# Hybrid recurrent decoder step: head loads on Pool's queue, one matmul per sample state instead of two, LayerNorm pieces on ACT and DVE alone

## The chip, the cores and the metric

The kernel runs on one core of a Trainium2 chip. The metric is the device time of one execution in microseconds. Three runs of the kernel before took 2374.15, 2374.71 and 2378.41 us; the median is 2374.71 us. The profiled execution, from which all durations below come, took 2384.39 us.

A core has five engines that each work through their own queue in program order: TensorE (PE, matrix products), VectorE (DVE), ScalarE (ACT), GpSimd (POOL) and SyncE (SP). SP and POOL also issue most DMAs here. An engine, or a queue, whose next instruction waits for something holds everything behind it.

## The reference, cut to what matters

One layer of a decoder is computed for a prompt (512 tokens) and for 8 sample tokens with states of their own. One projection `u @ w_in` (2048 x 19464) gives the columns of three mixers and of the gates:

- A: a gated linear recurrence, 8 heads with 128 x 128 states;
- B: retention, 4 heads with 256 x 256 states;
- C: mLSTM, 4 heads with 256 x 256 states.

Each branch is normalised per head, multiplied by a gate and projected by `w_branch`; the three are merged with sigmoid gates, projected by `w_out`, and `LayerNorm(alpha * x + out)` is the result. For a sample token of B (and, with other factors, C) one step is

```
s_new = chunk_dec[:, None, None] * s + jnp.einsum('bshk,bshv->bhkv', ..., vc)
o     = jnp.einsum('bthk,bhkv->bthv', ..., s_new)      # q^T S of the state after its update
```

So each of 8 tokens x 4 heads x 2 mixers = 64 states of 256 x 256 is loaded, updated, stored and multiplied by its q vector. The last step of the layer is `(h - mu) * rsqrt(var + eps) * ln_g + ln_b` over rows of 2048.

## The kernel before, in words

Dense products. All float32 matrices are split into a high and a low part (`hi`, `lo`, type float32r), and a product is hi*hi + hi*lo + lo*hi. The weights stream through three 1 MB buffers `R`; ACT makes `hi`, DVE makes `lo`. Work is cut into items: 24 matmuls of 128x260 for a Strassen product of `w_in`, 48 for an item of a plain product (the first three column blocks, `w_branch`, `w_out`). In most Strassen units two column blocks of the weights are summed by DMA into `TT`: SP loads the first, POOL adds the second with an accumulating DMA (`one.hook(2, ...)` in `strassen_unit`).

Side work. The heads of A, B and C, and the samples, are generators. `dense` emits a few matmuls, yields, and `side_step` then lets three queues of generators (`prepq`, `scanq`, `sampq`) each emit a step, if a model clock (`Clock`, written when the program is built) says that the step's inputs are there and that DVE and ACT are not more than 2.0 and 2.5 us behind the end of the current item (`clk.next`, set in `dense` to 2.87 us after the item's start, L735). So the order of each engine's instructions is fixed when the program is built, by the clock's costs (L152 to 163).

Loads of the side work. A finished column block is parked in DRAM (`parked`, POOL's queue). `ld` (L782) brings the block of one head back into a slot of `SL`, a buffer of 16 slots of 128x520; `b_head` loads the rotary tables (L1167) and `lds_` in `bc_samp` the sample states (L1265). All three issue on SP's queue, where the loads of `R` and of the first half of `TT` stand as well. POOL's queue has the stores, the parked blocks, the `TT` accumulations and the broadcast of the samples' v (`SL<-vs`).

Samples of B and C, `bc_samp` (L1244). A 256x256 state lies in a slot as 128 partitions x two halves of 256 columns; rows 2p and 2p+1 of the state share partition p. ACT multiplies v by k for both halves (`SL<-SL,ks`), DVE updates both halves, POOL stores the state, and PE forms q^T S as two float32 products of 128x256, one for each half, whose left side is q masked to the token's column (`qmask`, tile `qmt`), all 16 of a head accumulated in `os`.

Last LayerNorm, `norm_rows` (L1767). Rows are finished in two halves (two chunks of 128 rows each). Each chunk is cut into three or four pieces; a piece is scaled by ACT, multiplied by `g` on DVE, and `b` is added on POOL for the first two pieces and on DVE for the rest. The first half is a generator in `sampq`, emitted beside the last matmuls; the second half comes after them, interleaved with `norm_samples`.

## Time and profile before

| | |
|---|---|
| median of three runs | 2374.71 us (2374.15 to 2378.41) |
| profiled execution, device time | 2384.39 us |
| its span, first to last instruction | 2382.5 us |
| PE busy | 2318.9 us (97%) |
| DVE busy | 1603.2 us (67%) |
| ACT busy | 1031.3 us (43%) |
| POOL busy | 490.8 us (21%) |
| mean granted TensorE clock | 0.992 |

How to read it: `PD` are the accumulators of the dense products, `s` and `os` those of the side work and of the samples. A float32 matmul leaves two records in the trace, a float32r matmul or a transpose one; so the 128 products of the samples of B and C stand as 256 records. All engine operations are recorded by one wrapper and so have one line, L165; DMAs have L142, accumulating DMAs L143. The A heads run from about 180 to 800 us of the span, B from 800 to 1300, C from 1280 to 1793; the branch projections follow until about 2125, the output projection until 2353.6, and the rest is the LayerNorm of the second half.

### The profile page before, as it was taken

What the parts mean: (1) busy time and instruction counts of PE and PEld (TensorE: products, weight loads), DVE (VectorE), ACT (ScalarE), POOL (GpSimd) and SP (SyncE); (2) the same over time, 40 slices, a digit from 0 to 9 for tenths busy, and PEclk for the clock granted to TensorE, in tenths of its full rate; (3) what the DMA queues carried; (4) which work ended last, traced back from release to release, by engine and by line L of the source; (5) the groups of instructions that cost most, each with busy time, mean ns of one, the idle gap of its engine ahead of it and who ended that gap; (6) DMA issues with size and microseconds to landing.
All of it is one profiled execution on the core that took longest, in us unless ns stands there. A gap on an engine that the chain in (4) does not pass through costs nothing.

```text
span 2382.5 us, 45461 instructions
## 1 busy us (share of the span) xinstructions
PE 2318.9 (97%) x18677; PEld 2240.8 (94%) x18677; DVE 1603.2 (67%) x2571; ACT 1031.3 (43%) x1611; POOL 490.8 (21%) x653
## 2 busy tenths in 40 slices
PE   7999999999999999999999999999999999999995
PEld 7999999999999999999999899898999999999994
DVE  5777777787778868677777666767676534553336
ACT  4344445445545444454445545554554422222222
POOL 2022221323222132222122222212221100002002
PEclk9999999999999999999999999999999999999997
DMA  6367765647566576767767988889796767755221
GB/s 178 116 158 186 196 161 170 184 151 219 149 204 167 182 213 189 223 216 205 234 184 207 187 246 203 221 200 241 169 252 173 225 201 256 253 192 199 89 72 72
DMA packets 404690, 449.26 MB, mean 189 GB/s; under 512 B 16993, under 2 KB 356865, under 8 KB 402945
## 3 DMA queue, kind: packets, MB, share of 16 engines
q1 hardware_dynamic: 313664, 312.77, 42.3%
q0 software_dynamic: 90384, 133.38, 24.2%
q8 instruction: 147, 2.41, 0.4%
q14 instruction: 63, 0.51, 0.1%
q10 hardware_dynamic: 432, 0.20, 0.0%
HBM read 362.98 MB, written 83.28 MB: 187 GB/s over the span
## 4 chain that ended last, share of the span: by engine, by line
PE 61%; DMA 3%; DVE 1%; ACT 1%; issue 0%; POOL 0%; SPq 0%; DVEq 0%; POOLq 0%; ACTq 0%
PE PD L165 54%; PE s L165 4%; PE os L165 3%; DMA R<-in_w_in_dram 1%; DVE SL L165 1%; DMA out_dram<-SL 0%; DMA R<-in_w_branch_dram 0%; DMA TT<-in_w_in_dram 0%; ACT hi L165 0%; DVE lo L165 0%; ACT SL L165 0%; ACT TT L165 0%; DVE sdd L165 0%; DVE R L165 0%; DVE fmv L165 0%
## 5 line engine op out<-in xcount | busy, mean ns | idle before, releaser
L165 PE MATMUL PD<-XZ,hi 128*128 128x260 f32 x9920 | 1430.0, 285 | 13.3 <-ACT hi L165 10.0
L165 PEld LDWEIGHTS PD<-XZ,hi 128*128 128x128 f32 x9920 | 1282.7, 189 | 30.8 <-ACT hi L165 12.0
L165 DVE TENSOR_TENSOR lo<-R,hi 128x1024 fp32r<-128x1024 f32 (+1 forms) x540 | 646.1, 1198 | 381.2 <-ACT hi L165 161.6
L165 PE MATMUL PD<-XZ,lo 128*128 128x260 f32 x4944 | 799.4, 284 | 0.2 <-DVE lo L165 0.2
L165 ACT ACTIVATE hi<-R 128x1024 fp32r<-128x1024 f32 (+1 forms) x541 | 558.1, 1051 | 499.4 <-PE PD L165 254.8
L165 PEld LDWEIGHTS PD<-XZ,lo 128*128 128x128 f32 x4944 | 679.9, 189 | 5.5 <-issue 4.3
L165 ACT ACTIVATE SL<-PD 128x260 f32<-128x260 f32 x304 | 115.2, 381 | 424.3 <-PE PD L165 363.9
L165 POOL COPY smp<-SL 128x8 f32<-128x8 f32 x104 | 93.1, 895 | 535.3 <-ACT SL L165 344.2
L165 DVE TENSOR_TENSOR R<-R,R 128x1024 f32<-128x1024 f32 x146 | 178.0, 1219 | 6.4 <-DMA R<-in_w_in_dram 6.2
L165 DVE TENSOR_TENSOR SL<-SL 128x256 f32<-128x256 f32 (+9 forms) x315 | 146.4, 501 | 32.9 <-PE s L165 26.5
L165 PE MATMUL PD<-X,hi 128*128 128x260 f32 x1168 | 165.1, 287 | 0.3 <-ACT hi L165 0.3
L165 DVE TENSOR_TENSOR SL<-PD,SL 128x260 f32<-128x260 f32 x219 | 93.0, 425 | 99.4 <-PE PD L165 89.8
L165 PEld LDWEIGHTS PD<-X,hi 128*128 128x128 f32 x1168 | 148.4, 188 | 5.0 <-issue 4.1
L165 PE MATMUL s<-SL 128*128 128x64 f32 (+5 forms) x912 | 147.3, 298 | 0.0
L143 POOL DMA_DIRECT2D TT<-in_w_in_dram x56 | 90.2, 1610 | 272.7 <-DMA TT<-in_w_in_dram 245.5
L165 PEld LDWEIGHTS s<-SL 128*128 128x128 f32 (+1 forms) x912 | 125.0, 187 | 6.2
L165 ACT ACTIVATE SL<-SL 128x520 f32<-128x520 f32 (+5 forms) x156 | 85.2, 565 | 66.4 <-DVE SL L165 64.9
L142 POOL DMA_DIRECT2D out_dram<-SL x100 | 61.0, 614 | 217.9 <-DVE SL L165 196.3
L165 POOL TENSOR_TENSOR rstd<-rva,half 128x4 f32<-128x4 f32 (+3 forms) x35 | 45.2, 1292 | 247.5 <-DVE rva L165 247.4
L165 DVE TENSOR_TENSOR lo<-TT,hi 128x1024 fp32r<-128x1024 f32 x73 | 88.8, 1217 | 3.1 <-ACT hi L165 3.0
L165 DVE TENSOR_TENSOR R<-R 128x1024 f32<-128x1024 f32 x73 | 88.9, 1217 | 0.0
L165 PE MATMUL PD<-X,lo 128*128 128x260 f32 x584 | 84.7, 285 | 0.0
(213 smaller groups left out, 1416.7 us busy)
## 6 DMA issues: line engine op xcount, KB each, us to landing
R<-in_w_in_dram SPq DMA_DIRECT2D x150, 1024.0 KB, 6.3
TT<-in_w_in_dram SPq DMA_DIRECT2D x56, 512.0 KB, 6.4
TT<-in_w_in_dram POOLq DMA_DIRECT2D x56, 512.0 KB, 6.5
R<-in_w_branch_dram SPq DMA_DIRECT2D x24, 1024.0 KB, 6.5
out_dram<-SL POOLq DMA_DIRECT2D x88, 256.0 KB, 5.5
R<-in_w_out_dram SPq DMA_DIRECT2D x16, 1024.0 KB, 5.4
pk_g<-SL POOLq DMA_DIRECT2D x48, 260.0 KB, 4.7
SL<-pk_g SPq DMA_DIRECT2D x48, 260.0 KB, 5.9
```

What stands on the lines that cost most here:

```text
L142: return f(out=out, in_=in_)
L143: return f(out=out, in_=in_, accum_op=accum_op)
L165: return f(*a, **kw)
```

## The change

- `ld`, the rotary tables and the sample states are issued on POOL's queue instead of SP's: 32 + 40 + 40 loads of blocks and tables and 64 of states, 176 in all.
- In `bc_samp` the two halves are joined before the product: after the update ACT forms half 0 times q0 (per partition scalar) in a free slot, DVE adds half 1 times q1, and PE makes one 128x256 product whose left side is the constant mask `e8`. `qmask` goes for B and C.
- `norm_rows` has four pieces of 512 columns a chunk; DVE does both the product with `g` and the sum with `b`, ACT scales one piece ahead, and POOL has no piece. The generator's steps come due sooner (`clk.latest = 0.0`, `yield 1` instead of `yield 2`).
- Two numbers of the model clock: a float32 matmul costs twice as much, and an item of a plain product has 5.74 us to its end instead of 2.87 (Strassen items keep 2.87). Both change where side work is emitted.

```diff
-                    t = max(0.06, 0.00046 * n) if a[2].dtype == F32R else max(0.06, 0.00085 * n)
+                    t = max(0.06, 0.00046 * n) if a[2].dtype == F32R else 2 * max(0.06, 0.00085 * n)
...
-            clk.next = clk.pe + 2.87
+            clk.next = clk.pe + it.span
...
     def ld(nm, k, pre=False):
         s = sl()
-        SY.dma_start(out=v3(s[:, 0:S], 2), in_=d2(ptile(f"{nm}{k}"))[:, :, 0:256], pre=pre)
+        G.dma_start(out=v3(s[:, 0:S], 2), in_=d2(ptile(f"{nm}{k}"))[:, :, 0:256], pre=pre)
...
-            SY.dma_start(out=cs2[i][:, 0:S], in_=rope[i, :, 0:S])
+            G.dma_start(out=cs2[i][:, 0:S], in_=rope[i, :, 0:S])
...
-            SY.dma_start(out=v3(st[:, 0:512], 2), in_=state_in[0, b, h].rearrange("(p t) v -> p t v", t=2), pre=True)
+            G.dma_start(out=v3(st[:, 0:512], 2), in_=state_in[0, b, h].rearrange("(p t) v -> p t v", t=2), pre=True)
...
-        qm = [qmask(q[e], e) for e in range(2)]
...
-                fr(tm)
                 yield 1
                 for b in bs:
-                    st = lds.pop(b)
-                    for e in range(2):
-                        T.matmul(po[0:NS, 0:256], qm[e][:, b, :], st[:, e * 256:(e + 1) * 256],
-                                 start=(b == 0 and e == 0), stop=(b == 7 and e == 1))
+                    i = (b % 2) * 256
+                    act(out=tm[:, i:i + 256], in_=lds[b][:, 0:256], func=AF.Copy, scale=q[0][:, b:b + 1])
+                yield 1
+                for b in bs:
+                    i, st = (b % 2) * 256, lds.pop(b)
+                    V.scalar_tensor_tensor(out=tm[:, i:i + 256], in0=st[:, 256:512], scalar=q[1][:, b:b + 1],
+                                           in1=tm[:, i:i + 256], op0=MUL, op1=ADD)
                     fr(st)
+                yield 1
+                for b in bs:
+                    i = (b % 2) * 256
+                    T.matmul(po[0:NS, 0:256], e8[:, b, :], tm[:, i:i + 256], start=(b == 0), stop=(b == 7))
+                fr(tm)
                 yield 1
...
-        for c in range(2):
-            hh = H[:, c0 + c, :]
-            for q0, q1, e in (((0, 672, G), (672, 1344, G), (1344, 2048, V)) if c0 + c < 3 else
-                              ((0, 640, G), (640, 1152, G), (1152, 1600, V), (1600, 2048, V))):
-                qq = slice(q0, q1)
-                act(out=hh[:, qq], in_=hh[:, qq], func=AF.Identity, scale=r[:, c:c + 1], bias=nm[:, c:c + 1])
-                V.tensor_tensor(out=hh[:, qq], in0=hh[:, qq], in1=g[:, qq], op=MUL)
-                e.tensor_tensor(out=hh[:, qq], in0=hh[:, qq], in1=b[:, qq], op=ADD)
-                SY.dma_start(out=y_p[0, (c0 + c) * 128:(c0 + c + 1) * 128, qq], in_=hh[:, qq])
-                yield 2
+        pieces = [(c, slice(q0, q0 + 512)) for c in range(2) for q0 in range(0, D, 512)]
+
+        def scaled(c, qq):
+            hh = H[:, c0 + c, qq]
+            act(out=hh, in_=hh, func=AF.Identity, scale=r[:, c:c + 1], bias=nm[:, c:c + 1])
+
+        scaled(*pieces[0])
+        for i, (c, qq) in enumerate(pieces):
+
+            if i + 1 < len(pieces):
+                scaled(*pieces[i + 1])
+            hh = H[:, c0 + c, qq]
+            V.tensor_tensor(out=hh, in0=hh, in1=g[:, qq], op=MUL)
+            V.tensor_tensor(out=hh, in0=hh, in1=b[:, qq], op=ADD)
+            SY.dma_start(out=y_p[0, (c0 + c) * 128:(c0 + c + 1) * 128, qq], in_=hh)
+            clk.latest = 0.0
+            yield 1
```

How it moves instructions, at three places.

PE's queue at the end of the samples of the last C head, before (`PD` are dense matmuls, `os<-SL,qmt` the samples' products, x4 is two states):

```order
L165 MATMUL PD_126<-X_85,hi_121 128x260 x3
L165 MATMUL os<-SL,qmt 8x256 x4
L165 MATMUL PD_126<-X_85,hi_121 128x260 x13
L165 MATMUL PD_126<-X_85,lo_123 128x260 x8
L165 MATMUL PD_125<-XZ,hi_122 128x260 x3
```

and in the change:

```order
L165 MATMUL PD_127<-XZ,hi_120 128x260 x16
L165 MATMUL PD_127<-XZ,lo_123 128x260 x2
L165 MATMUL os<-SL,e_91 8x256 x2
L165 MATMUL PD_127<-XZ,lo_123 128x260 x6
L165 MATMUL PD_128<-X_85,hi_121 128x260 x16
```

Two states now take two products instead of four, and the left side is the constant mask.

SP's queue in the samples of the last but one C head, before (`R` are the weights, `SL<-in_state_mlstm_c` the states, `pk_mo` and `pk_mz` parked blocks):

```order
L142 DMA TT<-in_w_in_dram 128x8x128
L142 DMA SL<-in_state_mlstm_c_dram 128x512
L142 DMA SL<-pk_mo_12045 128x2x256
L142 DMA SL<-pk_mo_12146 128x2x256
L142 DMA SL<-pk_mz_12266 128x2x256
L142 DMA SL<-pk_mz_12374 128x2x256
L142 DMA SL<-in_state_mlstm_c_dram 128x512 x3
L142 DMA R_116<-in_w_in_dram 128x8x256
L142 DMA R_117<-in_w_in_dram 128x8x256
```

and POOL's queue in the samples of the last C head in the change (`pk_g` are parked gates, `out_dram<-SL` stores):

```order
L142 DMA SL<-pk_mo_13343 128x2x256
L142 DMA SL<-pk_mo_13466 128x2x256
L142 DMA SL<-pk_mz_13617 128x2x256
L142 DMA SL<-pk_mz_13728 128x2x256
L143 DMA TT<-in_w_in_dram 128x8x128
L142 DMA out_dram<-SL 128x512
L142 DMA pk_g_12_17483<-SL 128x520
L142 DMA SL<-vs_111 128x512
L142 DMA SL<-in_state_mlstm_c_dram 128x512 x2
L142 DMA SL<-vs_111 128x512
L142 DMA SL<-in_state_mlstm_c_dram 128x512
L142 DMA pk_g_13_17602<-SL 128x520
```

SP keeps the weights, the first halves of `TT` and the gates; the states and blocks now stand between POOL's stores and accumulations.

DVE's queue from the last tile of the output projection to the second half's statistics, before:

```order
L165 BN_STATS AT<-SL 128x6 x2
L165 TENSOR_TENSOR SL<-SL,lng 128x704
L165 TENSOR_TENSOR SL<-SL,lnb 128x704
L165 TENSOR_TENSOR SL<-SL,lng 128x672 x2
L165 TENSOR_TENSOR SL<-SL,lng 128x704
L165 TENSOR_TENSOR SL<-SL,lnb 128x704
L165 BN_AGGR fmv<-AT 128x2 x2
```

In the change ten operations of 512 columns, five with `lng` and five with `lnb` in turn, stand between the same two rows; these are the last of them:

```order
L165 TENSOR_TENSOR SL<-SL,lng 128x512
L165 TENSOR_TENSOR SL<-SL,lnb 128x512
L165 BN_AGGR fmv<-AT 128x2 x2
L165 TENSOR_SCALAR rva<-fmv 128x2
L165 SCALAR_TENSOR_TENSOR nm<-fmv,rstd 128x2
```

Three of the first half's eight pieces now stand ahead of the last tile, where two of six stood before.

More of the change, by code (lines that the diff above doesn't have):

```diff
@@ L327, in tile_hybrid_step @@
     e8 = const.tile([128, 8, 8], F32, name="e8")
-    qmt = const.tile([128, 2, 8, 8], F32, name="qmt")
+    qmt = const.tile([128, 8, 8], F32, name="qmt")
     ones = const.tile([128, 1], F32, name="ones")
@@ L425, in ralloc @@
         return r
+    span = [5.74]
     class Item:
@@ L433, in __init__ @@
             self.late = False
+            self.span = span[0]
             self.part = None
@@ L500, in strassen_unit @@
     def strassen_unit(col, deint, fin):
+        span[0] = 2.87
         src = w_in[0][:, col:col + 256]
@@ L654, in classical_rows @@
     def classical_rows(src, rws, xf, fin, pre=None):
+        span[0] = 5.74
         kt = 8 * rws
@@ L806, in put_ys, with qmask @@
         V.scalar_tensor_tensor(out=ysm[:, 8 * br + k, :], in0=psum, scalar=gains[:, br, k:k + 1], in1=z, op0=MUL, op1=MUL)
-    def qmask(q, e):
-        t = qmt[:, e]
-        V.tensor_tensor(out=t, in0=e8, in1=q.unsqueeze(2).to_broadcast([128, NS, 8]), op=MUL)
-        return t
+    def qmask(q):
+        V.tensor_tensor(out=qmt, in0=e8, in1=q.unsqueeze(2).to_broadcast([128, NS, 8]), op=MUL)
+        return qmt
     def samp_silu(i0, n):
@@ L1023, in a_samp @@
         hb = {}
-        qm = qmask(q, 0)
+        qm = qmask(q)
         def get(b0):
```

## The prediction

> **What bounds the kernel now.** I read the page's busy times first, then the stretches, then PE's waits, and last the queue of SP.
>
> ```profile
> span 2382.5 us, 45461 instructions
> PE 2318.9 (97%) x18677; PEld 2240.8 (94%) x18677; DVE 1603.2 (67%) x2571; ACT 1031.3 (43%) x1611; POOL 490.8 (21%) x653
> PE 61%; DMA 3%; DVE 1%; ACT 1%; issue 0%; POOL 0%; SPq 0%; DVEq 0%; POOLq 0%; ACTq 0%
> ```
>
> PE is busy for 97% of the span, and the chain that ended last is followed back over two thirds of the span with 61 of its 66 points on PE. The stretches show where the rest lies; columns are PE, weight loads, DVE, ACT, POOL, clock, DMA share, GB/s (the last row has PE alone of the engines).
>
> ```profile
> 50.00:450.00 400.00, 395.47 (x3308) 392.11 (x3307) 301.19 (x454) 178.73 (x288) 84.08 (x106) 1.00 0.59 160
> 450.00:800.00 350.00, 349.60 (x2889) 340.05 (x2889) 275.59 (x474) 171.61 (x303) 100.21 (x128) 1.00 0.62 176
> 800.00:1300.00 500.00, 498.95 (x3905) 472.16 (x3903) 368.53 (x552) 236.43 (x355) 125.24 (x172) 1.00 0.72 213
> 1300.00:1800.00 500.00, 488.96 (x3769) 457.17 (x3768) 348.78 (x595) 258.18 (x404) 112.70 (x146) 0.99 0.87 210
> 1800.00:2335.00 535.00, 530.29 (x4413) 527.58 (x4412) 250.70 (x379) 150.84 (x192) 39.66 (x69) 1.00 0.56 182
> 2354.00:2383.00 29.00, 1.12 (x4) 0.52 0.32 123
> ```
>
> PE idles 1 us in the B heads (800 to 1300), 11 us in the C heads (1300 to 1800), and 28 us after its last product. The clock is full. So a microsecond taken off PE's queue is a microsecond of the span, as long as DVE (70 to 79% busy there) and the loads keep up.
>
> **The products of the samples.** 64 of 128 products go.
>
> ```profile
> L165 PE MATMUL os<-SL,qmt 128*8 128x256 f32 x256 | 61.9, 380 | 0.0
> 1080.31 1.89 PE L165 MATMUL os<-SL,qmt 128*8 128x256 f32 x8
> 1082.13 0.98 PE L165 MATMUL PD<-XZ,lo 128*128 128x260 f32 x6
> ```
>
> The timeline has eight records, four products, from 1080.31 until the dense matmuls go on at 1082.13: 1.82 / 4 = 0.455 us each, 64 x 0.455 = 29.1 us. By the group's busy time it is 61.9 / 2 = 31.0. I take 29.1.
>
> **What they are replaced by.** For each of 64 states one ACT operation and one DVE operation of 256 columns; 16 `qmask` operations go.
>
> ```profile
> L165 ACT ACTIVATE SL<-SL,ks 128x256 f32<-128x256 f32 x128 | 62.2, 503 | 2.5 <-DMA SL<-vs 0.4
> L165 DVE SCALAR_TENSOR_TENSOR SL<-SL 128x256 f32<-128x256 f32 x64 | 22.9, 418 | 0.1
> L165 DVE TENSOR_TENSOR qmt<-e,smp 128x64 f32<-128x64 f32 x24 | 4.6, 218 | 0.0
> ```
>
> ACT gets 64 x 0.503 = 32.2 us, DVE 64 x 0.418 - 16 x 0.218 = 23.3 us. In 800 to 1800 DVE is idle for 1000 - 368.5 - 348.8 = 283 us and ACT for 505, so both fit under PE. They aren't free: a product now waits for a chain state update, ACT, DVE, and a `lo` operation queued behind a new one comes 0.4 us later. Without that cover all of DVE's 23.3 us would show. I take 4 us, between 0 and 12 (half of DVE's addition); nearer 0, because DVE has ten times the room.
>
> **SP's queue without the loads.** This is where the C heads' 11 us come from.
>
> ```profile
> SPq L142 <- DMA out_dram<-SL: 77.6, 17, 11.4
> 1605.33 1.37 SPq L142 DMA_DIRECT2D SL<-pk_mo  x2
> 1611.95 18.01 SPq L142 DMA_DIRECT2D SL<-in_state_mlstm_c_dram  x3
> 1630.01 1.05 SPq L142 DMA_DIRECT2D R<-in_w_in_dram  x2
> 1618.12 11.45 DMA out_dram<-SL
> 1630.01 6.43 DMA R<-in_w_in_dram
> 1636.47 1.06 ACT hi L165
> PE PD L165 <- ACT hi L165: 8.1, 4, 3.7
> ```
>
> A load of a state waits 11.45 us until the store out of its slot has landed, the weights behind it in the queue leave at 1630.01 and land 6.43 us later, ACT's `hi` comes at 1636.47, and PE has waited. In 1300 to 1800 PE has four such waits, 8.1 us, the longest 3.7. In the change the wait stands on POOL's queue and the weights leave when their buffer is free. I take 7 us, between 0 and 8.1.
>
> The Trainium skill, "DMA: Bandwidth & Descriptors", section "Issuing engines are not separate DMA queues", speaks against this: transfers from all issuing engines share the same 16 engines, and another issuer saves only issue time. By it this term is 0 and the rest of the sum stands; no run here shows it yet, since the rows above show a wait in a queue and not a want of bandwidth, though the DMA share of 0.87 allows either.
>
> **POOL's queue with them.** 176 loads come to a queue that waits on its own things.
>
> ```profile
> L143 POOL DMA_DIRECT2D TT<-in_w_in_dram x56 | 90.2, 1610 | 272.7 <-DMA TT<-in_w_in_dram 245.5 <-issue 16.5 <-DMA SL<-in_state_mlstm_c_dram 10.6
> L142 POOL DMA_DIRECT2D SL<-vs x48 | 26.5, 554 | 9.7 <-DVE SL L165 4.3 <-issue 3.7 <-PE s L165 0.7
> SL<-vs POOLq DMA_DIRECT2D x48, 256.0 KB, 5.8
> SL<-in_state_ret_dram SPq DMA_DIRECT2D x32, 256.0 KB, 7.6
> TT<-in_w_in_dram POOLq DMA_DIRECT2D x56, 512.0 KB, 6.5
> ```
>
> POOL's load is 176 x 0.554 = 97.5 us more, on 490.8: 25% of the span. A load of this size lands 5.8 us after its issue there and 7.6 on SP, where it follows 1 MB of weights; but POOL runs with PE and SP a little ahead of it, so I count arrival as equal. What is behind a waiting load: `TT` accumulations, and parked blocks whose slots are not short. What is ahead of a load: an accumulation that waits 272.7 / 56 = 4.9 us for its first half. In the changed order few loads stand right behind one. I take 1 us, between 0 and 6; a gain is excluded, since PE waits for none of these loads now.
>
> **The clock's numbers.** The dearer float32 matmul moves side work to places nearer to its inputs; that risk is in the 4 us above. The longer plain item lets the output projection's transposes of the second tile stand right behind the item's last matmul, where six matmuls of the next item stood between; the first tile's have stood so already.
>
> ```profile
> PE s L165 <- ACT TT L165: 2.5, 7, 0.4
> ```
>
> Seven times 0.36 us more: 2.5 us, between 2 and 4.
>
> **The LayerNorm.** From the last tile on, DVE is the chain.
>
> ```profile
> 2354.47 0.88 DVE L165 TENSOR_TENSOR SL<-SL,lng 128x704 f32<-128x704 f32 x1
> 2360.04 2.17 DVE L165 TENSOR_TENSOR SL<-SL,lnb 128x704 f32<-128x704 f32 x1
> 2362.14 1.02 DVE L165 BATCH_NORM_AGGREGATE fmv<-AT 128x2 f32<-128x96 f32 x2
> 2364.25 0.16 DVE L165 SCALAR_TENSOR_TENSOR nm<-fmv,rstd 128x2 f32<-128x2 f32 x1 [0.89 <-POOL rstd L165]
> 2378.59 0.62 DVE L165 TENSOR_TENSOR SL<-SL,lnb 128x448 f32<-128x448 f32 x1
> L165 DVE TENSOR_TENSOR SL<-SL 128x512 f32<-128x512 f32 x88 | 58.2, 684 | 1.4 <-ACT SL L165 1.4
> ```
>
> An operation of 704 columns takes 0.88 us alone and 2.17 beside POOL's `lnb`; POOL's pieces save DVE little. Before: 2354.47 to 2362.14, 7.7 us for the first half's rest; in the change ten operations of 512 at about 0.70 from start to start, 7.0. Second half, before: 2364.25 to 2379.21, 15.0 us. In the change: ACT's first piece 0.8, sixteen at 0.70, and the samples' small operations, about 2 us: 14.0. So 1.5 us less, between 0 and 3.
>
> **The sum.** -29.1 + 4 - 7 + 1 + 2.5 - 1.5 = -30.1 us on a span of 2382.5, so about 2352. The profiled execution's own time is 2384.4, the runs' median 2374.7, 10 us below it; the difference is taken from the median: 2374.7 - 30.1 = 2344.6, forecast **2345 us**. By the bounds: best -31.0 + 0 - 8.1 + 0 + 2 - 3 = -40.1, 2335; worst -29.1 + 12 + 0 + 6 + 4 + 0 = -7.1, 2368.
>
> **The rivals.**
>
> *The queue move is worth nothing*: the late weights were late for bandwidth. For it the DMA share of 0.87 in the C heads against 0.72 in B; against it the same 210 GB/s in both and the queue rows above. Then -23.1: 2352.
>
> *DVE becomes the bound in the samples*: with 23.3 us more it stands at 74% on average, but its work comes in bursts, and PE's queue waits in order. For it the chain of two more engines ahead of each product; against it only 1 us of PE idle at 74% in the B heads and 0.4 us at 79% in the A heads. All of DVE's addition showing: -29.1 + 23.3 + 2.5 - 1.5 = -4.8, 2370, no change or barely faster.
>
> *Slower: accumulations late on POOL's queue.* Each of 56 `TT` sums gets 176 / 56 = 3.1 loads ahead of it, 1.7 us; issued and landed it takes 1.6 + 6.5 = 8.1 us, and its first reader stands four items later. Four items of 24 matmuls at 68.37 / 569 = 0.12 us (2.88 us an item; both rows below) are 11.5 us, less the 4.9 us that it waits already: the slack is gone in many units. If each passes 1.7 us to PE, 56 x 1.7 = 95 us are added: 2440. It decides for slower from 30 / 1.7 = 18 of 56 on. Against it: ACT's `hi` waits for that DMA twice in the whole span, 1.4 us in all, and most loads don't stand right ahead of an accumulation.
>
> ```profile
> 1805.55 68.37 PE PD L165 x569
> ACT hi L165 <- DMA TT<-in_w_in_dram: 1.4, 2, 1.2
> ```
>
> **Chances.** Forecast 0.70, the queue move worth nothing 0.20, DVE the bound 0.05, accumulations late 0.05. The first two are faster whatever their size. What a measurement of this kernel can tell from no change is about 0.2%, 4.7 us; DVE's case lies at that edge and is shared. Faster 0.91, same 0.04, slower 0.05. Range 2333 to 2362: the forecast's bounds, with the first rival inside and the upper end cut where costs would all have to be at their worst.
>
> **What would show it.** PE's `os` products: 128 records of 128x256 where 256 were, about 30 us less busy. SP's row for waits on `out_dram<-SL` gone, and PE's idle time in the C heads down from 11 to a few us; were the first gone and the second not, the bandwidth rival is right. A row of ACT or PE waiting for `TT<-in_w_in_dram` of tens of us would show the slower rival. DVE's `lng` and `lnb` at 0.68 us each, and 1.5 us less from PE's last transposes to the end. The forecast is wrong if PE's idle time between 100 and 1800 grows by over 10 us.

## The result, and the profile after

| | before | after |
|---|---|---|
| median, same chip, four runs each | 2374.43 us (2372.87 to 2378.41) | 2441.98 us (2430.65 to 2447.98) |
| ratio | | 1.0276, 95% interval 1.0236 to 1.0316 |
| profiled execution / its span | 2384.4 / 2382.5 us | 2440.6 / 2438.8 us |
| mean granted TensorE clock | 0.992 | 0.983 |

The change is slower by 2.8%, 66 us; the forecast was 2345, 30 us faster. The head of the page of the changed kernel, and the engines of its chain:

```profile
span 2438.8 us, 45203 instructions
PE 2317.3 (95%) x18549; PEld 2247.7 (92%) x18549; DVE 1622.7 (67%) x2633; ACT 1058.4 (43%) x1678; POOL 570.9 (23%) x821
...
PE 77%; DMA 13%; DVE 4%; issue 3%; ACT 2%; POOL 1%; SPq 0%; ACTq 0%; DVEq 0%; POOLq 0%
```

DMA's share of the chain rises from 3 to 13%. The same stretches as before the change (PE, weight loads, DVE, ACT, POOL, clock, DMA share, GB/s):

```profile
50.00:450.00 400.00, 394.81 (x3298) 390.86 (x3298) 303.72 (x468) 185.16 (x306) 97.78 (x130) 1.00 0.59 162
450.00:800.00 350.00, 343.95 (x2829) 334.65 (x2828) 274.29 (x470) 166.36 (x287) 112.14 (x148) 1.00 0.63 181
800.00:1300.00 500.00, 484.38 (x3753) 463.06 (x3752) 365.99 (x562) 248.30 (x386) 153.41 (x233) 0.99 0.67 200
1300.00:1800.00 500.00, 461.35 (x3545) 441.34 (x3544) 336.99 (x553) 246.71 (x389) 135.17 (x192) 0.97 0.77 195
1800.00:2335.00 535.00, 521.71 (x4263) 512.68 (x4261) 265.44 (x411) 165.10 (x223) 59.18 (x98) 0.99 0.63 199
```

PE idles 6 us in 450 to 800 where it idled 0.4, 16 us in the B stretch (before 1) and 39 us in the C stretch (before 11), and the clock there is 0.97. DVE's busy time is no higher than before in any of these stretches but the first and the last: DVE is not what PE waits for. The products are as forecast:

```profile
L165 PE MATMUL os<-SL,e 128*8 128x256 f32 x128 | 34.5, 388 | 0.5 <-DVE SL L165 0.5
...
L165 DVE TENSOR_TENSOR SL<-SL,lnb 128x512 f32<-128x512 f32 x16 | 11.1, 692 | 0.6
L165 DVE TENSOR_TENSOR SL<-SL,lng 128x512 f32<-128x512 f32 x16 | 10.9, 683 | 1.0 <-ACT SL L165 0.9
```

The account of the 56.3 us between the two spans: PE's idle time rises by 58 us (63.6 to 121.5, span less busy time). Its busy time falls by 1.6 us only, though the time from start to start of the samples' products (`os<-SL`) falls from 74.7 to 47.5 us, by 27; the same remaining work takes about 25 us more. So 58 - 27 + 25 = 56. Two things are to be explained, idle time and a slower pace.

**Who PE waits for.** PE's and ACT's waits in the changed kernel (us in all, times, longest):

```profile
PE PD L165 <- ACT hi L165: 49.6, 25, 6.9
PE s L165 <- DMA SL<-pk_mo: 15.8, 8, 5.1
...
ACT hi L165 <- DMA R<-in_w_in_dram: 146.4, 52, 12.4
ACT hi L165 <- DMA TT<-in_w_in_dram: 21.5, 5, 7.8
```

Before, PE waited 10.3 us in all for ACT's `hi`, 7 times, and not for `pk_mo`; ACT's wait for the weights was this row:

```profile
ACT hi L165 <- DMA R<-in_w_in_dram: 59.1, 33, 3.8
```

Not all of this comes from the other queue. A kernel with the order of the change on PE, DVE and ACT, but with the 176 loads issued by SP (one of the four held-order kernels below), has these rows:

```profile
PE PD L165 <- ACT hi L165: 33.8, 15, 7.3
ACT hi L165 <- DMA R<-in_w_in_dram: 107.2, 47, 10.5
```

More than half of the rise is there already, with the order; the rest comes with the queue.

**One stall, followed back.** The longest, at 1502, in the timelines of PE, ACT, SP and POOL:

```profile
1500.83 1.13 PE L165 MATMUL PD<-XZ,lo 128*128 128x260 f32 x8
1508.81 3.84 PE L165 MATMUL PD<-XZ,hi 128*128 128x260 f32 x16 [6.85 <-ACT hi L165]
1512.44 1.30 PE L165 MATMUL PD<-XZ,lo 128*128 128x260 f32 x8
1513.58 2.08 PE L165 MATMUL PD<-XZ,hi 128*128 128x260 f32 x16
...
1507.70 1.06 ACT L165 ACTIVATE hi<-R 128x1024 fp32r<-128x1024 f32 x1 [12.40 <-DMA R<-in_w_in_dram]
...
1483.42 1.74 SPq L142 DMA_DIRECT2D R<-in_w_in_dram  x2
...
1484.19 1.07 POOL L142 DMA_DIRECT2D SL<-in_state_mlstm_c_dram  x2
...
1489.94 1.45 POOL L142 DMA_DIRECT2D SL<-pk_mv  x2
1491.38 1.44 POOL L142 DMA_DIRECT2D SL<-pk_mq  x2
1492.82 0.72 POOL L142 DMA_DIRECT2D SL<-pk_mk  x1
1494.04 0.72 POOL L142 DMA_DIRECT2D SL<-pk_mk  x1 [0.50 <-DMA pk_g<-SL]
```

The two loads of the weights leave SP in time, at 1483.4 and 1484.8; nothing in SP's queue holds them. The second lands at 1507.6, 22.8 us later, where the median of these loads is 6.6 us. Between 1482 and 1497 POOL sends off ten loads of 256 KB and four stores. The transfers of 1480 to 1510, by queue (packets, MB, share):

```profile
q1 hardware_dynamic: 3120, 2.62, 46.5%
q0 software_dynamic: 1190, 3.70, 36.3%
```

POOL's queue (q0) moved 3.7 MB beside the 2.6 MB of SP's (q1). That is not the whole of this stall: until 1502 the engines are busy, then they move 22 GB/s until the load has landed (the stretches further down), and the section on small stores comes back to this pause. The sharing, though, is found all through the B and C stretches. For the 78 loads of `R` issued between 800 and 1800 I counted from the trace what each queue moved between issue and landing:

```
time in flight   loads   mean us   POOL's queue   SP's queue   together
under 7 us          42       5.6        0.18 MB      1.36 MB   275 GB/s
7 to 9 us            9       7.8        0.58         1.98      328
9 to 12 us          17      10.0        1.11         2.01      311
over 12 us          10      16.0        2.53         2.21      297
```

The rate hardly changes; the time in flight follows the bytes of both queues (correlation 0.95). The ten slowest loads of the weights, which shared the transfer engines with 2.5 MB from POOL's queue on average, took 16 us; the 42 fastest took 5.6. These classes are picked by their outcome, and the step on average is smaller: in the change's order with the loads issued by SP, a load of the weights had 0.39 MB of POOL's queue beside it and took 7.5 us, 16 of 80 over 9 us; here it has 0.73 MB and takes 8.1 us, 27 of 78 over 9 us. The Trainium skill, "DMA: Bandwidth & Descriptors", section "Queues, rings and completion order", has a mechanism for it: each transfer engine takes turns between the queues that have work for it, packet by packet. The table agrees in that the bytes of both queues count; the turns themselves are not seen in it.

The heads' loads are late as well. At 1317 PE waits for `pk_mo`, whose load left POOL at 1311.94 behind an accumulation and two stores and took 10 us:

```profile
1306.69 1.59 POOL L143 DMA_DIRECT2D TT<-in_w_in_dram  x1 [4.76 <-DMA TT<-in_w_in_dram]
1310.80 1.43 POOL L142 DMA_DIRECT2D out_dram<-SL  x2 [2.52 <-DVE SL L165]
1311.94 1.47 POOL L142 DMA_DIRECT2D SL<-pk_mo  x2
...
1322.26 0.48 PE L165 MATMUL s<-ident,SL 128*128 128x128 f32 x1 [5.09 <-DMA SL<-pk_mo]
```

The second of the two stores writes 1 KB in 256 pieces of 4 bytes (`mn_p`, L1555 of the kernel before). While the two loads behind it are in flight the engines move 43 GB/s:

```profile
1314.00:1321.00 7.00, 3.17 (x27) 2.96 (x25) 3.07 (x4) 3.23 (x4) 2.33 (x4) 1.00 0.93 43
```

In all four C heads of the change the `pk_mo` loads stand on POOL's queue directly behind this store; before, on SP's queue, they leave 4 to 5 us ahead of it.

**The slower pace** stands in the first fence of the stall too: 16 matmuls take 3.84 us right after it and 2.08 us at 1513.58. The stretches around it, in the columns of above:

```profile
1490.00:1502.00 12.00, 10.06 (x69) 9.64 (x68) 3.21 (x7) 2.08 (x3) 5.18 (x7) 0.86 1.10 353
1502.00:1509.00 7.00, 0.19 (x1) 0.19 (x2) 1.38 (x2) 1.30 (x2) 0.00 (x0) 0.79 0.74 22
1509.00:1513.00 4.00, 4.00 (x20) 4.00 (x21) 2.81 (x3) 1.76 (x4) 1.57 (x1) 0.52 0.48 55
1513.00:1525.00 12.00, 12.00 (x104) 12.00 (x103) 6.83 (x10) 7.04 (x11) 1.29 (x4) 1.00 0.95 270
```

After the stall PE has 20 matmuls in 4 us at a granted clock of 0.52, then 104 in 12 us at 1.00. Most long stalls are paid twice. Between 50 us and the last dense product the trace's record of the clock has 2 stretches at half clock before and 13 in the change; PE is busy in them for 6.8 and 51.8 us. Half of that is lost, 3 and 26 us, which is 23 of the 25 us of slower pace.

### The profile page after: what moved, and what is told of

Its sections match the earlier page's. It is cut to its first block, busy times and chain, and to the rows that moved or that the text cites. A ratio compares the mean times of both kernels' runs of the same rounds, so it can differ in the third digit from the quotient of the medians.

```text
span 2438.8 us, 45203 instructions
## 1 busy us (share of the span) xinstructions
PE 2317.3 (95%) x18549; PEld 2247.7 (92%) x18549; DVE 1622.7 (67%) x2633; ACT 1058.4 (43%) x1678; POOL 570.9 (23%) x821
## 4 chain that ended last, share of the span: by engine, by line
PE 77%; DMA 13%; DVE 4%; issue 3%; ACT 2%; POOL 1%; SPq 0%; ACTq 0%; DVEq 0%; POOLq 0%
PE PD L165 68%; DMA R<-in_w_in_dram 9%; PE s L165 7%; PE os L165 2%; DMA SL<-pk_mo 2%; DVE SL L165 2%; DMA TT<-in_w_in_dram 1%; DVE lo L165 1%; ACT hi L165 1%; DVE R L165 1%; DMA R<-in_w_branch_dram 0%; ACT SL L165 0%; DVE XZ L165 0%; DMA SL<-in_x_prompt_dram 0%; ACT XZ L165 0%
## 5 line engine op out<-in xcount | busy, mean ns | idle before, releaser
L165 PE MATMUL PD<-XZ,hi 128*128 128x260 f32 x9920 | 1446.0, 287 | 53.2 <-ACT hi L165 49.3
L165 PEld LDWEIGHTS PD<-XZ,hi 128*128 128x128 f32 x9920 | 1296.0, 191 | 76.5 <-ACT hi L165 54.8
L165 POOL COPY smp<-SL 128x8 f32<-128x8 f32 x104 | 84.9, 817 | 469.4 <-ACT SL L165 287.8
L165 DVE TENSOR_TENSOR SL<-SL 128x256 f32<-128x256 f32 (+8 forms) x315 | 146.4, 500 | 38.9 <-PE s L165 26.5
L165 POOL TENSOR_TENSOR rstd<-rva,half 128x4 f32<-128x4 f32 (+3 forms) x35 | 36.5, 1044 | 280.3 <-DVE rva L165 271.9
L165 PE MATMUL s<-ident,SL 128*128 128x128 f32 x389 | 64.6, 284 | 26.8 <-DMA SL<-pk_mo 15.8
```

The costliest lines, as they stand in the source:

```text
L165: return f(*a, **kw)
```

## The experiments

Times differ by up to 0.5% between chips, so each ratio is to the kernel before on the same chip (its medians there: 2378.7 to 2386.7 us). Intervals are 95%. In us, a ratio is taken of 2378.7.

### Which part costs: one undone, three alone

Theory SHARED: the loads moved to POOL's queue cost it all, through the weights that land late. Rivals: the clock's numbers write a worse order (ORDER), or the longer chain ahead of the product holds PE up (JOINED). First the change with its loads back on SP:

```diff
-        G.dma_start(out=v3(s[:, 0:S], 2), in_=d2(ptile(f"{nm}{k}"))[:, :, 0:256], pre=pre)
+        SY.dma_start(out=v3(s[:, 0:S], 2), in_=d2(ptile(f"{nm}{k}"))[:, :, 0:256], pre=pre)
```

The rotary tables and the states go back likewise.

> The change with its 176 head loads back on SP's queue; all its other parts stay. Theory SHARED (the weights leave in time but land late, because the head loads on POOL's queue now run at the same time on the same transfer engines, and each stall costs PE a few us at a low clock besides): the 57 us of PE idle time and the lower clock go, about 2442 - 90 = 2345 to 2360 us, the R loads' share of waits back to about 59 us on ACT. Theory ORDER (the dearer float32 matmul and the longer plain item make the program's order worse, the loads do no harm): still 2430 to 2450. Theory JOINED (the longer chain ACT, DVE, product holds up PE or the weights' splitting): still 2430 or more.

The kernel before with these three lines on POOL's queue and nothing else:

> The kernel before with its 176 head loads on POOL's queue and nothing else. SHARED: slower by what it costs in the change, 2374 + 70 to 95 = 2445 to 2470 us, with ACT's waits for R<-in_w_in_dram over 120 us (59 before) and PE's for ACT hi over 40 us (10 before). ORDER and JOINED: within 10 us of 2374. My forecast's term for it: 2374 - 7 + 1 = 2368.

The kernel before with the changed `qmask` and the changed end of `bc_samp`:

> The kernel before with the joined product alone. SHARED: the 64 products less are a gain, 2374 - 29 + 0 to 12 = 2345 to 2357 us. JOINED: 2400 or more. ORDER: as SHARED.

The kernel before with the two numbers of the clock:

> The kernel before with the clock's two numbers alone (float32 products counted twice as dear, 5.74 us for a plain item). SHARED: within 10 us of 2374 (my term: +2.5). ORDER: 2420 or more.

| kernel | median us | ratio to before | in us |
|---|---|---|---|
| change, loads back on SP | 2369.27 | 0.9959 (0.9944 to 0.9973) | -10 |
| loads alone | 2434.12 | 1.0229 (1.0208 to 1.0249) | +54 |
| joined product alone | 2374.08 | 0.9976 (0.9965 to 0.9986) | -6 |
| clock's numbers alone | 2407.91 | 1.0118 (1.0101 to 1.0135) | +28 |

The loads are the largest part, but SHARED does not stand as it was written: the clock's numbers cost 28 us alone, where it expected less than 10, and the joined product gains 6 of the 17 to 29 it expected. SHARED's own figures are missed as well: the loads alone cost 54 us and not 70 to 95, with 98 us of waits of ACT for the weights and not over 120, and with the loads back ACT still waits 80 us for them and not 59. ORDER's 2420 for the clock's numbers is not reached either. And the parts don't add: joined product and clock's numbers, -6 and +28, are -10 together with the LayerNorm. Where it comes and goes is seen when two executions are compared at the same piece of dense work. Each kernel has 613 `lo` operations on DVE in the same sequence; the table has how much later than in the kernel before the n-th of them (counted from 0) starts, in us:

```
n (start before)   change   loads alone   loads back   joined   clock's numbers
220 ( 768.0)        17.5          3.3         17.9      -0.6          19.2
360 (1262.9)        19.9         10.2         -4.9     -17.7          23.5
500 (1768.1)        43.0         38.9        -13.4     -39.2          25.3
540 (1903.9)        54.4         50.5        -17.0     -13.9          19.3
612 (2327.1)        60.7         50.5        -11.9     -10.6          25.5
```

The loads cost in B and C. The clock's numbers cost by the end of the A heads, where my sum had nothing for them, and once more in the output projection (54.4 to 60.7), where it had. The joined product is 39 us ahead late in C and gives 25 us back between the 500th and the 540th `lo`. In that piece PE has 20.3 us of side work where the kernel before has 6.0, so 14 us are side work put off, and its idle time is 10 us longer, most of it one wait for `pk_mo`:

```profile
PE s L165 <- DMA SL<-pk_mo: 10.1, 2, 8.4
```

### Bytes, queue or number of issues

SHARED against POOLQ (what costs is the standing in POOL's queue: waits behind accumulations, the issues). The loads-alone kernel with a quarter of the bytes, and the kernel before with the same cut as a control; the rows of every engine stay in their places:

```diff
-        n = 4
+        n = 16 if out.shape[0] == 32 else 4
...
-        G.dma_start(out=v3(s[:, 0:S], 2), in_=d2(ptile(f"{nm}{k}"))[:, :, 0:256], pre=pre)
+        G.dma_start(out=v3(s[0:32, 0:S], 2), in_=d2(ptile(f"{nm}{k}"))[0:32, :, 0:256], pre=pre)
```

The rotary tables and the states are cut likewise, and in the control the same lines on `SY`. The clock goes on booking whole loads.

> The loads-only kernel (2434 us) with each of its 176 moved loads cut to 32 of 128 partitions, a quarter of the bytes; the program's order on every engine is the same row for row. It leaves out three quarters of what these loads fetch, so the heads compute on stale data. SHARED (the weights land late because the moved loads' bytes share the transfer engines with them): back to 2370 to 2390 us, ACT's waits for R<-in_w_in_dram from 98 us to under 70. POOLQ (the cost is in POOL's queue itself: accumulations and loads standing behind waiting ones, the number of issues): 2415 or more, since all 176 issues and their order stay.

> The control: the kernel before (loads on SP) with the same cut to a quarter of the bytes, order unchanged, the same part left out. SHARED: little to gain where the loads stood in line with the weights: 2365 to 2376 us. If it gains as much as the cut on POOL's queue gains, the bytes cost the same on either queue and SHARED is wrong about the overtaking.

The quarter on POOL's queue took 2398.20 us, 1.0086 (1.0065 to 1.0108); the control on SP's 2375.66, 0.9985 (0.9976 to 0.9995). The cut is worth 34 us (1.43%) on POOL's queue and 4 us on SP's. ACT's wait for the weights falls with it, from this row of the loads-alone kernel

```profile
ACT hi L165 <- DMA R<-in_w_in_dram: 98.2, 42, 11.2
```

to this one:

```profile
ACT hi L165 <- DMA R<-in_w_in_dram: 75.8, 38, 7.8
```

So bytes cost on the second queue and next to nothing in line with the weights, as SHARED has it, and the time is well below POOLQ's 2415. It is also above SHARED's 2370 to 2390, and ACT's 75.8 us above its 70: 20 us stay that neither explains.

A third queue, filled by ACT (`A.dma_start` in the three lines):

> The loads-only kernel with the 176 loads issued by ACT in place of POOL: a third queue, filled by hardware. SHARED: the weights are overtaken all the same, 2415 us or more (ACT's own waits for slots may add to it). POOLQ: 2370 to 2390, since nothing stands behind POOL's accumulations any more, unless ACT's rows show waits for slots of over 20 us.

It took 2423.05 us, 1.0180 (1.0155 to 1.0205), and not for either theory's reason:

```profile
ACT hi L165 <- DMA R<-in_w_in_dram: 58.9, 32, 6.2
ACT SL L165 <- DMA out_dram<-SL: 28.9, 5, 11.2
```

The weights are waited for no longer than before (58.9 against 59.1 us); ACT itself stands still for slots whose stores haven't landed, and the planner's order is another one again. This run does not tell the theories apart.

Only the loads of the states (one line on POOL's queue). The expectation miscounts them: they are 64 of the 176, 16 of 44 MB.

> The kernel before with only the 128 loads of the samples' states of B and C on POOL's queue; the heads' own loads stay on SP. SHARED: the states are 32 MB of the 44 MB moved, but go two at a time; the bursts are the heads' loads (up to nine of 256 KB at once in C): about a third of the 55 us, 2385 to 2400. My forecast's term (the wait on out_dram<-SL leaves SP): 2367 to 2374.

2387.32 us, 1.0037 (1.0022 to 1.0052): 64 loads cost 9 us, so by difference the 112 loads of blocks and tables, which come up to six in a row, cost some 46, the order that comes with them included. PE's idle time in 1300 to 1800 does fall with it, from 11 to 8 us, as my term for SP's queue had it, though by 3 us and not 7, and 800 to 1300 loses as much:

```profile
800.00:1300.00 500.00, 496.01 (x3871) 468.46 (x3870) 367.01 (x546) 233.71 (x352) 141.16 (x199) 1.00 0.72 209
1300.00:1800.00 500.00, 491.89 (x3816) 459.91 (x3816) 351.28 (x603) 262.14 (x410) 133.51 (x185) 1.00 0.84 214
```

### The planner's answer, held apart from the queue

The clock books a load on the engine that issues it. Told that POOL has 176 more, it writes another order for PE, DVE and ACT too. New theory REACTION: the 20 us are this order. Four kernels have all rows of PE, DVE and ACT in the order of another kernel and differ from it only in the issuing queue. The trick is a handle that issues on one engine and books on the other:

```diff
-    G, SY = Counted(nc.gpsimd, "pool", clk), Counted(nc.sync, "sp", clk)
+    G, SY, GB = Counted(nc.gpsimd, "pool", clk), Counted(nc.sync, "sp", clk), Counted(nc.gpsimd, "sp", clk)
...
-        SY.dma_start(out=v3(s[:, 0:S], 2), in_=d2(ptile(f"{nm}{k}"))[:, :, 0:256], pre=pre)
+        GB.dma_start(out=v3(s[:, 0:S], 2), in_=d2(ptile(f"{nm}{k}"))[:, :, 0:256], pre=pre)
```

The rotary tables and the states likewise; for the reverse the handle is `Counted(nc.sync, "pool", clk)`.

The order of the kernel before, loads on POOL's queue:

> The 176 loads issued by POOL, but booked by the clock as SP's, so that PE, DVE and ACT have row for row the order of the kernel before; only the issuing queue differs. SHARED (bytes of two queues at once make the weights late): still slow, 2405 to 2440 us, with R loads in the C heads in flight for 9 us on average and ACT's waits for them 90 us or more. REACTION (what costs is that the planner, told of a busier POOL, puts the side work elsewhere): 2370 to 2385. The quarter of the bytes left 20 us unexplained; if this comes out near 2415, those 20 are the reaction.

The order of the loads-alone kernel, loads on SP's queue, and the order of the change, loads on SP's queue:

> The loads-only kernel's order (booked on POOL by the clock: PE, DVE and ACT row for row as in it) with the 176 loads issued by SP. REACTION (the order that the planner writes for a busier POOL is worse by itself): 2374 + 25 to 35 = 2400 to 2415 us. SHARED TWICE (the order costs only where two queues run at once, since it sends the loads in closer bursts): within 10 us of 2374.

> The whole change, its order row for row on PE, DVE and ACT, but the 176 loads issued by SP. By REACTION: about 30 us over the loads-back kernel (2369), 2395 to 2410 us. By SHARED TWICE: 2365 to 2380.

The order of the loads-back kernel, loads on POOL's queue:

> The loads-back kernel's order (2369 us) with the 176 loads issued by POOL: only the queue differs. The same step in the order of before cost 24 us: 2369 + 20 to 30 = 2389 to 2399 us if the cost of the queue does not hang on the order; 2420 or more if the joined product's order makes it dearer.

| order of PE, DVE and ACT | loads issued by SP | loads issued by POOL | the queue's cost |
|---|---|---|---|
| kernel before | 1 | 1.0098 (1.0074 to 1.0122) | 23 us |
| written for loads on POOL, rest as before | 1.0078 (1.0043 to 1.0112) | 1.0229 (1.0208 to 1.0249) | 36 us |
| change's other parts, written for loads on SP | 0.9959 (0.9944 to 0.9973) | 1.0105 (1.0063 to 1.0146) | 35 us |
| the change | 1.0077 (1.0051 to 1.0103) | 1.0276 (1.0236 to 1.0316) | 47 us |

Not every size came out as expected. In the order of the kernel before, the time on POOL's queue, 2404, lies between the two theories' ranges: the weights are 9.0 us in flight in the C heads, as SHARED said (8.4 in the kernel before, where 23 of 40 landings are on record), but ACT waits 74 us for them and not 90. The loads-alone order on SP's queue costs 19 us where REACTION said 26 to 41. The queue in the loads-back order costs 35 us, above the 20 to 30 and below the dearer case (51 or more).

Read across, the queue itself costs 23 to 47 us, always. Read down the SP column, the order that the clock writes when it is told of loads on POOL costs 19 us (1 to 1.0078) and 28 us (0.9959 to 1.0077) even when the loads are not there. REACTION holds, beside SHARED and not in its place, and SHARED TWICE, which had the order harmless on SP's queue, falls. The change: -10 (its other parts) + 28 (order) + 47 (queue) = +65; that this is the whole is no check, since each step is the difference of two neighbouring kernels.

The quarter of the bytes falls into place with it. It has the loads-alone order, in which the queue costs 36 us; the cut gives back 34 of them, and the 20 us that stayed are the 19 of the order. So it is the bytes that cost on POOL's queue, hardly the number of issues.

Where PE loses them is seen in the profiles of the four pairs (us, loads on SP to loads on POOL; waits between 50 and 2340 us):

| order | span | PE idle | waits for ACT's `hi` | waits for loads into `SL` | PE busy at half clock |
|---|---|---|---|---|---|
| kernel before | +20 | 64 to 76 | 10 to 13 | 0 to 6 | 7 to 17 |
| written for loads on POOL | +27 | 80 to 101 | 26 to 36 | 1 to 10 | 26 to 36 |
| change's other parts | +40 | 74 to 95 | 20 to 17 | 0 to 15 | 8 to 42 |
| the change | +37 | 96 to 122 | 34 to 50 | 7 to 16 | 36 to 52 |

The rise of PE's idle time and half of the rise of its time at half clock make up nearly the whole of each difference. But the late weights, of which PE learns by waiting for `hi`, are the larger part in two orders only; in the other two it is the heads' own loads, `pk_mo` above all, that come late. How much of that second part is the small store ahead of them was not tested.

Why the written order is worse is not settled. In the loads-alone order on SP's queue the four longest stalls between 1500 and 1760 (2.7 to 5.4 us) each wait for a load of `R` that was 12 to 16 us in flight, and in the first and the third of these flights the transfer engines all but stop (next but one section); that is an observation on one profile.

### The clock's numbers

```diff
-                    t = max(0.06, 0.00046 * n) if a[2].dtype == F32R else max(0.06, 0.00085 * n)
+                    t = max(0.06, 0.00046 * n) if a[2].dtype == F32R else (2 if n < 256 else 1) * max(0.06, 0.00085 * n)
```

> The kernel before with the dearer float32 price for products of fewer than 256 columns only, plain items unchanged. The A heads use only such products. If the loss of the clock's numbers is the A heads' order (17 to 19 us by the 220th splitting of the weights) it is all here: 2374 + 15 to 25 = 2390 to 2400 us. If it is the 256-column products of the samples and of B and C: within 8 us of 2374.

2409.47 us, 1.0130 (1.0115 to 1.0145), more than the 2390 to 2400 expected. The dearer price of the small products alone costs as much as both numbers of the clock together (1.0118). Its lateness is 14.3 us at the 220th `lo` and 22.6 at the end, so the A heads have most of it and not all. The price is the truer one (a float32 matmul leaves two records, 0.455 us for 256 columns where the old price says 0.218), and the order it gives is worse.

### A pause after small stores

In the second row of the stretches around the stall at 1502 the transfer engines move 22 GB/s, with two loads of weights in flight. The same is in the kernel before, with no stall behind it:

```profile
1560.00:1574.00 14.00, 14.00 (x119) 13.84 (x119) 10.13 (x21) 8.65 (x15) 3.83 (x7) 1.00 0.72 152
1574.00:1583.00 9.00, 9.00 (x64) 7.88 (x62) 4.16 (x8) 6.97 (x13) 1.10 (x2) 1.00 0.92 52
1583.00:1590.00 7.00, 7.00 (x57) 6.87 (x56) 4.01 (x6) 2.72 (x5) 0.00 (x0) 1.00 0.92 293
```

The DMA share is 0.92 and 52 GB/s move. Ahead of it stands a store of the samples' n, `out_dram<-nt`, 8 KB in 1024 pieces of 8 bytes:

```profile
1572.31 0.92 POOL L142 DMA_DIRECT2D out_dram<-nt  x1 [5.38 <-DVE qmt L165]
```

In the change such a pause stands clearly behind two of the four stores (1496 and 1696); the one at 1502 follows this:

```profile
1496.20 0.92 POOL L142 DMA_DIRECT2D out_dram<-nt  x1 [1.44 <-DVE kn L165]
```

Both kernels with that store cut to 8 partitions, order held:

```diff
-            G.dma_start(out=mn_s[0, :, h].rearrange("b (p t) -> p b t", t=2), in_=nt)
+            G.dma_start(out=mn_s[0, :, h].rearrange("b (p t) -> p b t", t=2)[0:8], in_=nt[0:8])
```

> The change, order unchanged, with the four stores out_dram<-nt (1024 pieces of 8 bytes each) cut to 8 of 128 partitions; it leaves out the rest of that output. Some 3 us after each of these stores the transfer engines move under 60 GB/s for 5 us, with weights in flight. PAUSE (the 8-byte store holds up the weights, and with the loads on POOL's queue the weights have no slack left for it): 2442 - 10 to 25 = 2417 to 2432 us. If the pause has another cause or is hidden: 2437 to 2445.

> The control: the kernel before, order unchanged, with the same cut of the four stores out_dram<-nt (8 of 128 partitions, the rest of that output left out). If the pause costs only where the weights have lost their slack: 0 to 6 us less than before (ratio 0.9975 to 1.0). If it costs the same in both kernels: 12 to 20 us less (0.992 to 0.995), and the pause is no part of what the change costs.

The change with the cut: 2430.31 us, 1.0191 (1.0153 to 1.0230), against 2441.98 and 1.0276 whole; the two ran on different chips, so the gain is about 12 us by the medians and 20 by the ratios, whose intervals leave 7 to 33. At the stall of 1502 the second load of the weights takes 17.9 us instead of 22.8 and PE waits 3.2 us instead of 6.9. The kernel before with the cut: 2378.16, 0.9988 (0.9979 to 0.9997), 3 us. So four stores of 8 KB cost 3 us in the kernel before and several times as much in the change, where the weights are late more often. Whether that belongs to the queue's 47 us or to the order's 28 no run tells: the cut was not tried in the change's order with the loads on SP.

These are not the only stores of this kind. The four of 256 pieces of 4 bytes (`mn_p`), of 1 KB each, are 8 to 15 us in flight and are followed by the same pause, in the kernel before too: after the one at 1483.6 under 50 GB/s are moved from 1488.6 to 1495.6. The two pauses of the loads-alone order on SP's queue stand behind them (1502.4 and 1661.7), and so does the wait of 11.45 us for a store on which my term for SP's queue rested (the one at 1609.8). No run changes them.

### The parts that gain, together

> The joined product and the LayerNorm pieces with the loads on SP, the dearer price for products of 256 columns and more only, plain items at 2.87 us. If the A heads' 18 us and the out-projection's 4 us are what the clock's numbers cost in the loads-back kernel (2369): 2369 - 22 = 2345 to 2352 us, faster than both. If the parts don't add: 2360 to 2375.

> The same without any of the clock's numbers: joined product (2374 alone) and LayerNorm pieces, loads on SP. The LayerNorm by my term -1.5: 2370 to 2374 us. The difference to the kernel with the 256-column price shows what that price is worth to the joined product.

| kernel, loads on SP | median us | ratio to before |
|---|---|---|
| joined, LayerNorm, dear price from 256 columns | 2369.09 | 0.9961 (0.9947 to 0.9975) |
| joined, LayerNorm, clock as before | 2370.07 | 0.9960 (0.9949 to 0.9971) |
| joined, LayerNorm, the change's clock (loads back) | 2369.27 | 0.9959 (0.9944 to 0.9973) |

The 22 us that I meant to save by leaving the A heads' price alone don't come: with the joined product three orders give one time. Last, the first of them with the small stores made into rows of 1 KB:

```diff
-            G.dma_start(out=mn_s[0, :, h].rearrange("b (p t) -> p b t", t=2), in_=nt)
+            p = ps()
+            for e in range(2):
+                T.transpose(p[0:NS, e * 128:(e + 1) * 128], nt[:, :, e], ident)
+            w = small.tile([NS, 128, 2], F32, tag="nw", name="nw", bufs=1)
+            act(out=w.rearrange("b p t -> b t p"), in_=v3(p[0:NS, 0:256], 2), func=AF.Copy)
+            G.dma_start(out=mn_s[0, :, h], in_=w.rearrange("b p t -> b (p t)"))
```

> The joined product and the LayerNorm pieces with the loads on SP and the 256-column price (2369 us, 0.9961), and the four 8-byte stores turned into rows of 1 KB by two transposes and one ACT operation each. By the pause: 5 to 15 us less, 2355 to 2364. Every edit moves the planner's order, which was worth 19 to 29 us in three kernels: 2350 to 2385 is possible.

2363.70 us, 0.9941 (0.9927 to 0.9954): 14 us faster than before and 3.3% faster than the change. Against the kernel that it starts from the rows are worth 5 us by the ratios, at the lower end of what was expected, and the two intervals overlap. Its C stretch has 9 us of idle time at full clock:

```profile
1300.00:1800.00 500.00, 490.73 (x3846) 465.81 (x3845) 372.02 (x638) 282.97 (x454) 107.13 (x153) 1.00 0.83 218
```

## Why the prediction was wrong, point by point

**The bound.** "A microsecond taken off PE's queue is a microsecond of the span, as long as DVE and the loads keep up" failed by its condition: I tested DVE's half of it and not the loads'. Even with the loads left on SP's queue, 27 us off PE's queue gave 6 us alone and 10 with the LayerNorm.

**Products, -29.1.** Right: 27 us by the `os` records from start to start. The chain ahead of them cost PE little directly (its `os` waits for DVE rose from 2.4 to 4.4 us). But alone the joined product nets 6 us, since the order that comes with it has other waits, 8.4 us for one `pk_mo` among them. The term of 4 us (0 to 12) for the cover was too small: about 21 us are lost. It was a price for the chain; that the rest is the price of a redrawn order is my reading, as no run holds the order here.

**SP's queue without the loads, -7, and POOL's queue with them, +1.** This is the step that failed: instead of -6 the two are +47, and +28 for the order that comes with them. SP's wait for `out_dram<-SL` is gone, and "the weights leave when their buffer is free" holds. What fell is what I took from it, that they then land in 6.4 us, and on POOL's side "I count arrival as equal": the states do arrive as before, but the median of the `pk_mo` loads goes from 6.8 to 10.6 us, and PE, which waited for none of them, now waits 15.8 us. The wait in SP's queue was also not where the C heads' 11 us come from. With a quarter of the bytes on SP's queue SP still waits 67.4 of the 77.6 us for these stores, but PE idles 3 us there instead of 11, and waits 3.7 us for `hi` instead of 10.3: so the weights were late for bytes before the change too. In one queue the loads of the heads stand in line with the weights, and SP's own waits space them; as I now read it, the 77.6 us of waits that I counted as a nuisance were also what kept 256 KB loads from running beside 1 MB of weights. On two queues they run at the same time, and the time in flight of both grows with the bytes of the other queue.

**The rule of the skill.** The Trainium skill, "DMA: Bandwidth & Descriptors", section "Issuing engines are not separate DMA queues", says that transfers from all engines run on the same 16 engines and interleave. I took from it that another issuer gains nothing (2352, the first rival). That what interleaves is also delayed is an inference that I did not draw; the turns packet by packet of the section "Queues, rings and completion order" on that page of the Trainium skill point the same way. The runs bear it out: a quarter of the bytes gives back 34 of the queue's 36 us.

**The clock's numbers, +2.5.** In the output projection, where I costed them, the lateness grows by 6 us from the 540th `lo` to the last, and 2 of them come back after it (51.0 against 53.1 us, below): 4 us, at the end of my bounds. "That risk is in the 4 us above" was the mistake: alone the dearer price of the small products costs 31 us, more than half of it by the end of the A heads, which I did not look at because nothing of the change's code is there. In the company of the joined product the clock's numbers cost nothing (2369 with them, 2370 without).

**LayerNorm, -1.5.** Right. From the last `lo` to the end the kernel before takes 55.4 us and the two with the new LayerNorm and loads on SP 53.1 (clock as before) and 51.0 (the change's clock): 2.3 us less by the LayerNorm itself. `lng` and `lnb` take 0.68 and 0.69 us.

**The rivals.** The third, accumulations late on POOL's queue, named 2440, and the time is 2442: the number is right by accident. Its sign was there, a row of ACT waiting for `TT<-in_w_in_dram` of 21.5 us, but beside 146.4 us for `R`, which never passes through POOL; with the loads on SP in the same order it is 6.1. It decided by issues in a queue; with all 176 issues in place and a quarter of the bytes most of the cost is gone. "DVE becomes the bound" is refuted by the stretches. The first rival had the want of bandwidth right, and its sign came (SP's row gone, PE's idle time not down), but it put the price at nothing.

**The chances.** 0.91 for faster rested on the claim that the signs of all large terms were known. What the profile had against it: a DMA share of 0.87 in the C heads, where I moved traffic, and weights for which ACT already waited 33 times, up to 3.8 us, which I had not shown. Both say that the weights have little slack there. My own sign of being wrong, 10 us more of PE's idle time, was passed in the B and C heads alone (12 to 54 us). The lower end of the range, 2333, lies 2 us below the bound of 2335 that it was taken from.

## What to carry to other kernels

A queue that makes transfers wait is also a priority: before moving loads to another queue, ask which urgent transfer they now run beside, and add their bytes to its time in flight. Look at the slack of that transfer (how late and how often its reader waits already), not at the waits of the queue that is relieved. Where a planner writes the order, an edit has two effects, the work and the order; hold the order while you measure the work, for here orders of the same work differed by 19 to 31 us.

## What the runs showed of the hardware

- **Half a clock after a stall of 2 us.** In the twenty profiles of this study, between 50 us and the last dense product, 83 of 94 stalls of PE of 2 us or more (33 of 42 between 2 and 3 us, all 31 over 4) and 24 of 161 of 1 to 2 us have a stretch of half clock beginning in them or within 3.5 us behind them. The stretches last 3.4 us or two or three times that, and a dense matmul then takes about 216 ns from start to start instead of 120. The Trainium skill, "TensorE: Matmul & The Clock Gate", section "What's actually happening", has the clock at half after an idle window of about 3.4 us; the length of the stretches agrees with it, but here shorter stalls were enough.
- **A pause of the transfer engines after stores of 4-byte and 8-byte pieces**: 22 to 52 GB/s for 7 to 9 us in the stretches shown, with the DMA share at 0.74 to 0.93. Without four of these stores the kernel before is 3 us faster and the change 12 to 20.
- **The same load of 1 MB, 5.6 or 16 us**: in flight it shares a rate of 275 to 328 GB/s with what else was issued, from either queue.
